# Float32r groups by single tiles, the first group copied out unnormalised, LayerNorm's tail in stages

## The chip, the cores and the metric

The kernel runs on one core of a Trainium2 chip. The metric is the device time of one execution in microseconds (us). Engines are TensorE (PE, matmuls; PEld is its weight load), VectorE (DVE), ScalarE (ACT), GpSimd (POOL) and SyncE (SP, which here only issues transfers). All run their own instruction streams in order and wait for each other by semaphores.

## The reference, cut to what matters

One layer on x of 512 tokens by 2048 channels, all in float32:

```
h = rms_norm(x) ; z = h @ w_in            # 2048 -> 7 x 1024
u = a_val * sigmoid(a_glu)                # mixer A
u = causal_depthwise_conv(u, width 31)
u = silu(layer_norm(u)) @ conv_pw_w + conv_pw_b ; y_a = u * silu(a_gate)
q, k = per-head rms_norm ; o = dilated_window_attention(q, k, v)   # 16 heads of 64
y_b = o * silu(b_gate)                    # mixer B
out = x + concat(y_a, y_b) @ w_out
```

## The kernel before, in words

Activations lie with channels on the 128 partitions and the 512 tokens along the row (x is passed transposed), so a matmul is 128x128 weights against 128x512 activations into one bank of PSUM. `GROUPS` lists 28 groups of 512 output columns. A *unit* is one group's weights for `KU` = 4 tiles of 128 input rows (1 MB), loaded into one of `RING` = 6 buffers `raw`. Units run in order; a group keeps four banks (`lin_ps`), m = 0 to 3, one for each 128 of its columns, and is evacuated (`evac`) when its last unit is done.

Each product is made of three matmuls on operands split in a high and a low part (`tri`, L361 to L365): high by high, high by low, low by high. From unit 8 on the parts are float16 of scaled weights (`split_hi` on ScalarE, `split_lo` on VectorE, one unit ahead) and of normalised x (`x16`, from `norm_x`). The first two groups (`vg` 0 and 1, units 0 to 7: conv value and gate columns) come before the row of 1/rms is known: their parts are float32r, of the raw weights (`exact_hi` L268, `exact_lo` L274) and of x times the norm's gain (`split_x` L311: hh and hl for even k, xr for odd). They are made two tiles of 128 rows at a time, half a unit ahead of use, in `PARTS` = 2 buffers, which the float16 parts use afterwards. These groups' banks are multiplied by `rrow` (1/rms of each token) on the way out (`evac_vg` L379).

Order is written out by hand. The time is counted in *steps* (`clock`): each unit has eight, and a step issues six matmuls. Before a step's matmuls the program emits what `after(n, fn)` has put into `calendar` for it, and the extras of that unit (`startup` L760 for units 0 to 7). Within an engine instructions run in the order of emission. The squares for the 1/rms are summed in `square_x`, turned into `rrow` by `token_rsqrt` (small matmuls L347, a power on GpSimd, a diagonal matrix on VectorE, a matmul L357); `norm_x` makes x16 afterwards.

The convolution and the LayerNorm behind it are a generator (`conv` L465). `run_conv` (L699) resumes it in a step when the planner's load of VectorE (180 plus the row length for each instruction, less `PACE` = 1200 a step) is below zero; the generator's `yield n` asks for n steps of rest. Its LayerNorm: sum of the eight tiles, mean by a matmul (L490), differences and squares, `token_rsqrt`, and a loop in which tile i is multiplied by 1/sigma (VectorE), goes through SiLU with gain and bias (ScalarE, L518), and tile i-2 is split into the float16 parts u16 (`split16` L296). The pointwise groups `pw` need all of u16. The attention heads run through the calendar at the same time: scores in three `s_ps` banks (L574, L575), exponentials on ScalarE (L584), values (L612). The scale of each later group's weights comes from sums of squares on ScalarE (`measure`, L182) and a small matmul (`bound`, L194).

At the start, SP issues all transfers in one list (L733 to L753): w tile 0, x0, w tile 1, x1, w tiles 2 and 3, x2 to x5, w tiles 4 and 5, and so on; GpSimd's queue loads the two gains qg and kg broadcast to 128 partitions (`load_consts` L147). Before the first real work `WARM` = 8 matmuls on zeros run.

Of the kernel before, what the change touches and what calls it, by code (L numbers as in the profile page):

```python
# [25 lines left out]
TAPS = 31  # L26
DH = 64
RING = 6
PARTS = 2
FIRST = 2  # L30
SLOTS = 37
LP = 4
WARM = 8
KU = 4
PERIOD = {0: 16, 1: 22}
START = 180
NORM_FROM = 32
PACE = 1200
RMS_EPS = 1e-6
LN_EPS = 1e-5  # L40
# [35 lines left out]
def layer(ctx: ExitStack, tc: tile.TileContext, xt, w1, w2, w3, g_in, conv_w, conv_b,  # L76
# [35 lines left out]
    def after(n, fn):  # L112

        calendar.setdefault(clock[0] + max(n, 1), []).append(fn)
# [32 lines left out]
    def load_consts():  # L147
        for t, src in ((cw, conv_w), (cb, conv_b), (lng, ln_g), (lnb, ln_b), (pwb, pw_b), (tab, table)):
            nc.sync.dma_start(t, src)
        for t, src in ((qg, q_g), (kg, k_g)):  # L150
            nc.gpsimd.dma_start(t, src.partition_broadcast(P))

# [112 lines left out]
            if i == mine[-1]:  # L265
                after(4, lambda: bound("w", sums.pop(group), lambda s, v: wscale.update({group: (s, v)})))

    def exact_hi(i, h, cuts=(0, 2)):  # L268

        wt = parts[i, h] = part_pool.tile([P, 2, 2, S], R32, name="wr", tag="part")  # L270
        for a, b in zip(cuts, cuts[1:]):
            A.activation(wt[:, 0, a:b], raw[i][:, 2 * h + a:2 * h + b], AF.Copy)

    def exact_lo(i, h, cuts=(0, 2)):  # L274
        wt = parts[i, h]
        for a, b in zip(cuts, cuts[1:]):
            V.tensor_tensor(wt[:, 1, a:b], raw[i][:, 2 * h + a:2 * h + b], wt[:, 0, a:b].bitcast(F32), op=OP.subtract)
        if h == 1:
            raw.pop(i)
            load(i + RING)  # L280
            after(max(9, 25 - 4 * i), lambda: measure(i + RING))

    def split_hi(i):
        if i < len(units):
            wt = part_pool.tile([P, 2, KU, S], F16, name="w16", tag="part")
            A.activation(wt[:, 0], raw[i], AF.Copy, scale=wscale[units[i][3:]][0])  # L286
            parts[i] = wt

    def split_lo(i):
        if i < len(units):  # L290
            wt = parts[i]
            V.scalar_tensor_tensor(wt[:, 1], raw.pop(i), wscale[units[i][3:]][0], wt[:, 0], op0=OP.mult, op1=OP.subtract)
            load(i + RING)
            after(9, lambda: measure(i + RING))

# [35 lines left out]
    def norm_x(k):  # L331

        t = temp("xn")
        V.scalar_tensor_tensor(t, xraw.pop(k), gs[:, k:k + 1], rrow, op0=OP.mult, op1=OP.mult)
        n = slots.tile([P, 2, S], F16, name="x16", tag="slot")
        A.activation(n[:, 0, :], t, AF.Copy)
        x16[k] = (n[:, 0, :], n[:, 1, :])
        after(2, lambda: V.tensor_tensor(n[:, 1, :], t, n[:, 0, :], op=OP.subtract))

    rstd = const.tile([P, NT], F32, name="rstd")  # L340
    rrow = slot("rrow")
# [37 lines left out]
    def evac_vg(g, m, ps):  # L379

        i = 2 * g + m // 2
        if m % 2 == 0:
            t = glu[i] = temp("glu")
            if g < FIRST:
                V.tensor_mul(t, ps, rrow)
                A.activation(t, t, AF.Sigmoid)
            else:
                A.activation(t, ps, AF.Sigmoid, scale=evac_scale(("vg", g)))
        else:
            t = u[i] = slot("u")  # L390
            if g < FIRST:
                V.tensor_mul(t, ps, rrow)
                V.tensor_mul(t, t, glu.pop(i))
            else:
                V.scalar_tensor_tensor(t, ps, evac_scale(("vg", g)), glu.pop(i), op0=OP.mult, op1=OP.mult)
# [69 lines left out]
    def conv():  # L465
# [27 lines left out]
        A.activation(mean_sb, mean, AF.Copy, scale=1.0 / C)  # L493
        yield 2
        acc2 = slot("lnacc2")
        sq = None
        for i in range(8):
            V.tensor_sub(cv[i], cv[i], mean_sb)
            if sq is not None:
                V.tensor_add(acc2, acc2, sq)  # L500
            if i == 0:
                A.activation(acc2, cv[i], AF.Square)
            else:
                sq = temp("lnsq")
                A.activation(sq, cv[i], AF.Square)
            yield 1
        yield 2
        V.tensor_add(acc2, acc2, sq)
        yield 5
        c = small.tile([P, NT], F32, name="lncol")  # L510
        row = temp("lnrow")
        for _ in token_rsqrt(acc2, C, LN_EPS, c, row):
# [2 lines left out]
        for i in range(8 + 2):  # L515
            if i < 8:
                V.tensor_mul(cv[i], cv[i], row)
                A.activation(cv[i], cv[i], AF.Silu, scale=lng[:, i:i + 1], bias=lnb[:, i:i + 1])  # L518
            if i >= 2:
                u16[i - 2] = split16(cv.pop(i - 2), scales["u"][0], "u16")  # L520
            yield 3


    pair, swapped, outs = {}, {}, {}
# [182 lines left out]

    banks = {}

    def slot_matmuls(i, m, half_i):  # L710

        kind, g = group = units[i][3:]
        first_u, last_u = i == of_group[group][0], i == of_group[group][-1]
        if first_u and half_i == 0:
            banks[group, m] = lin_ps.tile([P, S], F32, name="ps_l")
        ps = banks[group, m]
        ms = slice(m * P, (m + 1) * P)
        exact = i < n_exact
        wt = parts[i, half_i] if exact else parts[i]
        for kk in range(2):  # L720
            wk = kk if exact else 2 * half_i + kk
            k = units[i][2] * KU + 2 * half_i + kk
            act = xr[k] if exact else (u16 if kind == "pw" else y16 if kind in OUT_K else x16)[k]
            first, last = first_u and half_i == kk == 0, last_u and half_i == kk == 1
            if kind in ("q", "k", "v"):
                tri(ps, (act[0][:, ms], act[1][:, ms]), (wt[:, 0, wk, :], wt[:, 1, wk, :]), first, last)
            else:
                tri(ps, (wt[:, 0, wk, ms], wt[:, 1, wk, ms]), act, first, last)
        if last_u and half_i == 1:
            return lambda: evac(group, m, banks.pop((group, m)))  # L730

# [3 lines left out]
        load_part(0, k, k + 1)  # L735
        fetch_x(k)
    load_part(0, 2, 4)
    for k in range(2, 6):
        fetch_x(k)
    load(1, (0, 2))  # L740
    for k in range(6, 10):
        fetch_x(k)
    load_part(1, 2, 4)
    for k in range(10, 13):
# [6 lines left out]
    load_consts()  # L751
    for i in range(4, RING):
        load(i)  # L753
    exact_hi(0, 0, (0, 1, 2))
    exact_lo(0, 0, (0, 1, 2))
    split_x(0)
    split_x(1)
    square_x(0)

    def startup(h):  # L760

        lists = [[], [], [], []]
        if h < 7:
            lists[0].append(lambda: split_x(2 * h + 2))
            lists[2].append(lambda: split_x(2 * h + 3))
        for n, k in enumerate(k for k in range(1, KC) if (k - 1) * 6 // 15 == h):
            lists[n % 4].append(lambda k=k: square_x(k))
        i, hf = divmod(h + 1, 2)
        if h < 15:
            lists[0].append(lambda: exact_hi(i, hf))  # L770
            lists[1].append(lambda: exact_lo(i, hf))
        else:
            lists[1].append(lambda: split_lo(n_exact))
        if h == 14:
            lists[3].append(lambda: split_hi(n_exact))
        if h == 6:
            g = token_rsqrt(xacc, D, RMS_EPS, rstd, rrow)
            for n in (0, 1, 3):
                lists[n].append(lambda: next(g, None))
        if h == 4:  # L780
            lists[1].append(x_consts)
        if h == 5:
            lists[3].append(score_consts)
        if h == 9:
            lists[1].append(u_consts)
        for k in range(KC):
            n = NORM_FROM + k * (56 - NORM_FROM) // KC
            if n // 4 == h:
                lists[n % 4].append(lambda k=k: norm_x(k))
        return lists  # L790

    for i in range(len(units)):
        kind, g = group = units[i][3:]
        exact = i < n_exact
        if exact:
            order = [(m, hf) for hf in range(2) for m in range(4)]
            extra = startup(2 * i) + startup(2 * i + 1)
        else:
            order = [(m, hf) for m in range(4) for hf in range(2)]
            extra = [[] for _ in range(8)]  # L800
            extra[0].append(lambda: split_hi(i + 1))
            extra[2].append(lambda: split_lo(i + 1))
            if i + 1 < len(units) and units[i + 1][3] == "wb":
                for m in range(4):
                    extra[2 * m].append(lambda m=m: fetch_res(4 * units[i + 1][4] + m))
        if kind == "pw" and i == of_group[group][0]:
            while 7 not in u16:
                next(convolution)
        for n, (m, hf) in enumerate(order):
            clock[0] = 8 * i + n  # L810
            for fn in calendar.pop(clock[0], []) + extra[n]:
                fn()
            run_conv()
            done = slot_matmuls(i, m, hf)
            if done:
                done()
        if kind == "k" and i == of_group[group][-1]:
            attention(g)
# [47 lines left out]
```

## Time and profile before

| | us |
|---|---|
| median of 3 runs (lowest, highest) | 858.41 (856.31, 859.18) |
| the profiled execution | 856.66 |
| its span, first to last instruction | 854.7 |

The profile is of one execution. Busy shares of the span: PE 98%, VectorE 70%, ScalarE 58%, GpSimd 13%. In the chain of work that ended last PE has 95%. In rows of instructions the form is: engine, source line, operation, output<-inputs by the program's names, size. All VectorE instructions carry L71, the line of the helper that weighs them. A wait is put down to the instruction that came last before it ended.

### The profile page before, as it was taken

The numbers are of one execution on the slowest core, as the hardware profiler recorded it, in microseconds if no ns is written. First come the engines' busy times: TensorE is split into PE (matmuls) and PEld (weight loads), VectorE is DVE, ScalarE is ACT, GpSimd is POOL, SyncE is SP. The second block draws the span as 40 slices with busy tenths as digits, with TensorE's granted clock in tenths as the row PEclk, the third lists the DMA queues.
The fourth block names the chain that finished last, engine by engine and source line by source line (L and its number), as shares of the span: only waits on it lengthen the run. The fifth ranks groups of instructions, "written<-read, shape, count | busy, mean of one in ns | idle before, by whom it ended". The sixth has DMA issues, their size and how long they took to land.

```text
span 854.7 us, 10860 instructions
## 1 busy us (share of the span) xinstructions
PE 841.8 (98%) x4157; PEld 426.0 (50%) x4157; DVE 602.4 (70%) x968; ACT 499.6 (58%) x654; POOL 114.1 (13%) x165
## 2 busy tenths in 40 slices
PE   8999999999999999999999999997999999999998
PEld 5878744444444444444444444443444444444443
DVE  5778689888898988788787767536537577545353
ACT  6647554443645466668667667868777774544110
POOL 0010010101413011004222102010101010111100
PEclk9999999999999999999999999999999999999999
DMA  9922322232353534443737543423335565341022
GB/s 311 349 80 75 144 99 99 99 110 101 103 167 90 169 118 134 105 117 102 199 115 173 154 130 87 142 94 86 114 121 137 169 225 166 106 122 50 2 99 98
DMA packets 79748, 110.24 MB, mean 129 GB/s; under 512 B 62256, under 2 KB 62640, under 8 KB 70480
## 3 DMA queue, kind: packets, MB, share of 16 engines
q1 hardware_dynamic: 78320, 107.24, 40.6%
q0 software_dynamic: 1088, 2.16, 1.0%
q8 instruction: 32, 0.52, 0.2%
q14 instruction: 20, 0.16, 0.1%
q10 hardware_dynamic: 288, 0.14, 0.1%
HBM read 88.56 MB, written 4.19 MB: 109 GB/s over the span
## 4 chain that ended last, share of the span: by engine, by line
PE 95%; ACT 3%; DMA 1%; issue 1%; DVE 1%; SPq 0%; DVEq 0%; ACTq 0%
PE ps_l L363 30%; PE ps_l L364 30%; PE ps_l L365 30%; PE ps_o L612 2%; PE ps_s L574 1%; PE ps_s L575 1%; DMA x<-xt_dram 1%; ACT junk L182 0%; ACT cv L518 0%; ACT u L299 0%; ACT sx L584 0%; DVE w L71 0%; ACT w L286 0%; DVE cv L71 0%; ACT gate L404 0%
## 5 line engine op out<-in xcount | busy, mean ns | idle before, releaser
L286 ACT ACTIVATE w<-wf,ws 128x2048 f16<-128x2048 f32 x68 | 136.1, 2002 | 169.8 <-PE ps_l L365 167.1
L71 DVE SCALAR_TENSOR_TENSOR w<-wf,ws,w 128x2048 f16<-128x2048 f32 x68 | 159.7, 2349 | 40.5 <-ACT w L286 40.4
L71 DVE SCALAR_TENSOR_TENSOR cv<-u,cw,cv 128x511 f32<-128x511 f32 (+14 forms) x240 | 160.2, 730 | 0.3 <-ACT cv L472 0.3
L364 PE MATMUL ps_l<-w,x 128*128 128x512 f16 x384 | 145.5, 379 | 0.0
L365 PE MATMUL ps_l<-w,x 128*128 128x512 f16 x384 | 145.5, 379 | 0.0
L365 PE MATMUL ps_l<-x,w 128*128 128x512 f16 x384 | 145.5, 379 | 0.0
L364 PE MATMUL ps_l<-x,w 128*128 128x512 f16 x384 | 145.5, 379 | 0.0
L363 PE MATMUL ps_l<-w,x 128*128 128x512 f16 x384 | 145.5, 379 | 0.0
L363 PE MATMUL ps_l<-x,w 128*128 128x512 f16 x384 | 145.5, 379 | 0.0
L182 ACT ACTIVATE junk<-wf 128x2048 bf16<-128x2048 f32 x68 | 129.2, 1900 | 2.3 <-DMA wf<-w_dram 2.1
L365 PEld LDWEIGHTS <-w 128*128 128x128 f16 x704 | 68.8, 98 | 83.1
L363 PEld LDWEIGHTS <-w 128*128 128x128 f16 x704 | 68.9, 98 | 82.1 <-issue 3.5
L364 PEld LDWEIGHTS <-w 128*128 128x128 f16 x704 | 68.8, 98 | 77.3 <-issue 0.7
L365 PE MATMUL ps_l<-y,w 128*128 128x512 f16 x256 | 97.0, 379 | 0.0
L364 PE MATMUL ps_l<-y,w 128*128 128x512 f16 x256 | 97.0, 379 | 0.0
L363 PE MATMUL ps_l<-y,w 128*128 128x512 f16 x256 | 97.0, 379 | 0.0
L71 DVE SCALAR_TENSOR_TENSOR res<-ps_l,esc,res 128x512 f32<-128x512 f32 (+1 forms) x49 | 36.0, 737 | 59.2 <-PE ps_l L365 51.4
L196 POOL TENSOR_SCALAR ws<-ws 128x1 f32<-128x1 f32 x26 | 9.4, 362 | 462.8 <-DVE ws L71 462.8
L365 PEld LDWEIGHTS <-x 128*128 128x128 f16 x384 | 37.6, 98 | 45.3
L363 PEld LDWEIGHTS <-x 128*128 128x128 f16 x384 | 37.6, 98 | 43.0
L364 PEld LDWEIGHTS <-x 128*128 128x128 f16 x384 | 37.6, 98 | 42.5
L71 DVE CUSTOM_DVE_ANT_0 sx<-ps_s,tab 128x128 f32<-128x128 f32 (+1 forms) x64 | 30.7, 487 | 33.3 <-PE ps_s L575 18.5
(185 smaller groups left out, 1044.6 us busy)
## 6 DMA issues: line engine op xcount, KB each, us to landing
wf<-w_dram SPq DMA_DIRECT2D x72, 1024.0 KB, 4.9
x<-xt_dram SPq DMA_DIRECT2D x16, 256.0 KB, 6.6
res<-xt_dram SPq DMA_DIRECT2D x16, 256.0 KB, 5.4
out_dram<-res SPq DMA_DIRECT2D x15, 256.0 KB, 2.0
wf<-w_dram SPq DMA_DIRECT2D x7, 512.0 KB, 7.2
kb<-k POOLq DMA_DIRECT2D x32, 64.0 KB, 3.8
wf<-w_dram SPq DMA_DIRECT2D x2, 256.0 KB, 3.7
tab<-table_dram SPq DMA_DIRECT2D x1, 256.0 KB, 4.0
```

The costliest lines, as they stand in the source:

```text
L71: return getattr(self.engine, name)(out, src, *args, **kw)
L182: A.activation(junk[:, :n], src, AF.Square, scale=scale, accum_out=acc)
L196: G.tensor_scalar(scale, scale, 1e-30, 2.0 ** (-2 * top), op0=OP.max, op1=OP.mult)
L286: A.activation(wt[:, 0], raw[i], AF.Copy, scale=wscale[units[i][3:]][0])
L363: T.matmul(ps, ah, bh, start=first, stop=False)
L364: T.matmul(ps, ah, bl, start=False, stop=False)
L365: T.matmul(ps, al, bh, start=False, stop=last)
L574: T.matmul(ps[:, :w], q[:, i * P:w], k[:, :w], start=True, stop=False)
L575: T.matmul(ps[:, :w], q[:, i * P:w], swapped[hd][:, :w], start=False, stop=True)
L612: T.matmul(po[:, i * P:(i + 1) * P], v2[j // 2][:, j % 2, h8, :], got["t"][:, part * (ALL // P) + FROM[i] // P + j, :], start=(j == 0 and ...
```

## The change

The float32r groups go by single tiles. Tile n is one weight tile (unit n // 4, row block n % 4) with high and low part in one of four buffers of half the size; the float16 units use two of these, one for each part. `exact_matmuls(n)` issues half a tile's twelve matmuls in a step, so a tile takes two steps: all high by high, then high weight by low x, then low weight by high x, over the four banks in turn; for the first and last tile of a group (but not the very first) it is sorted by bank instead. Parts of tile s+3 and x of tile s+2 are made in the steps of tile s. At the start weights and x alternate: tile 0, x0, tile 1, x1, tile 2. In SP's list w tiles 4 and 5 come ahead of x4 and x5. The broadcast loads of qg and kg go to step 12, the other pieces of the start get their own steps, and the normalising of x runs from step 37 to 70 instead of 32 to 56, with its high part a step after the multiplication and the low part a step later than it was. Nine warming matmuls.

The first group is copied out of its banks by ScalarE as it is; seven steps later it is multiplied by `rrow`, nine steps later comes the sigmoid, eleven later the product u. The second group is unchanged.

In LayerNorm the running sum stays two squares behind instead of one, with more rest between, and in the last loop SiLU follows one stage behind the multiplication, and the split two steps after that.

```diff
-PARTS = 2
+PARTS = 4
-WARM = 8
+WARM = 9
-NORM_FROM = 32
+NORM_FROM = 37
...
+    def exact_hi(n):
+        i, k = divmod(n, KU)
+        wt = parts[i, k] = part_pool.tile([P, 2, S], R32, name="wr", tag="part")
+        A.activation(wt[:, 0], raw[i][:, k], AF.Copy)
+    def exact_lo(n):
+        i, k = divmod(n, KU)
+        wt = parts[i, k]
+        V.tensor_tensor(wt[:, 1], raw[i][:, k], wt[:, 0].bitcast(F32), op=OP.subtract)
+        if k == KU - 1:
             raw.pop(i)
             load(i + RING)
-            after(max(9, 25 - 4 * i), lambda: measure(i + RING))
+            after(max(6, 25 - 4 * i), lambda: measure(i + RING))
...
+            parts[i] = [part_pool.tile([P, KU, S], F16, name=n, tag="part") for n in ("wh", "wl")]
+            A.activation(parts[i][0], raw[i], AF.Copy, scale=wscale[units[i][3:]][0])
...
-        after(2, lambda: V.tensor_tensor(n[:, 1, :], t, n[:, 0, :], op=OP.subtract))
+        after(1, lambda: A.activation(n[:, 0, :], t, AF.Copy))
+        after(3, lambda: V.tensor_tensor(n[:, 1, :], t, n[:, 0, :], op=OP.subtract))
...
+        if g == 0:
+            t = u[i, m % 2] = temp("glu") if m % 2 == 0 else slot("u")
+            A.activation(t, ps, AF.Copy)
+            def finish():
+                V.tensor_mul(t, t, u.pop((i, 0)))
+                u[i] = u.pop((i, 1))
+            after(7, lambda: V.tensor_mul(t, t, rrow))
+            if m % 2 == 0:
+                after(9, lambda: A.activation(t, t, AF.Sigmoid))
+            else:
+                after(11, finish)
...
-            if sq is not None:
-                V.tensor_add(acc2, acc2, sq)
+            if len(squares) > 1:
+                V.tensor_add(acc2, acc2, squares.pop(0))
...
+            yield 1 + i % 2
+        while squares:
             yield 1
-        yield 2
-        V.tensor_add(acc2, acc2, sq)
-        yield 5
+            V.tensor_add(acc2, acc2, squares.pop(0))
+        yield 4
...
                 V.tensor_mul(cv[i], cv[i], row)
-                A.activation(cv[i], cv[i], AF.Silu, scale=lng[:, i:i + 1], bias=lnb[:, i:i + 1])
+            if 1 <= i < 8 + 1:
+                A.activation(cv[i - 1], cv[i - 1], AF.Silu, scale=lng[:, i - 1:i], bias=lnb[:, i - 1:i])
+            yield 2
             if i >= 2:
                 u16[i - 2] = split16(cv.pop(i - 2), scales["u"][0], "u16")
-            yield 3
+            yield 1
...
+    def exact_matmuls(n):
+        s, second = divmod(n, 2)
+        i, kk = divmod(s, KU)
+        k = s % KC
+        group = units[i][3:]
+        wt, xk = parts[i, kk], xr[k]
+        terms = [(m, a, b) for a, b in ((0, 0), (0, 1), (1, 0)) for m in range(4)]
+        if s and k in (0, KC - 1):
+            terms = sorted(terms)
+        for m, a, b in terms[6 * second:][:6]:
+            if k == 0 and a == b == 0:
+                banks[group, m] = lin_ps.tile([P, S], F32, name="ps_l")
+            T.matmul(banks[group, m], wt[:, a, m * P:(m + 1) * P], xk[b], start=k == 0 and a == b == 0,
+                     stop=k == KC - 1 and a == 1)
+            if k == KC - 1 and a == 1:
+                evac(group, m, banks.pop((group, m)))
...
-    for k in range(2, 6):
+    for k in range(2, 4):
         fetch_x(k)
     load(1, (0, 2))
-    for k in range(6, 10):
+    for k in range(4, 10):
...
-    exact_hi(0, 0, (0, 1, 2))
-    exact_lo(0, 0, (0, 1, 2))
-    split_x(0)
-    split_x(1)
+    for n in range(2):
+        exact_hi(n)
+        exact_lo(n)
+        split_x(n)
+    exact_hi(2)
+    exact_lo(2)
     square_x(0)
...
+    def startup(n):
+        s, second = divmod(n, 2)
+        todo = []
+        if not second:
+            if s + 3 < KU * n_exact:
+                todo += [lambda: exact_hi(s + 3), lambda: exact_lo(s + 3)]
+            if s + 2 < KC:
+                todo.append(lambda: split_x(s + 2))
+        if n == 0:
+            for k in range(1, KC):
+                after(4 + (k - 1) * 26 // 14, lambda k=k: square_x(k))
+            for k in range(KC):
+                after(NORM_FROM + k * (70 - NORM_FROM) // KC, lambda k=k: norm_x(k))
+            g = token_rsqrt(xacc, D, RMS_EPS, rstd, rrow)
+            for m in (32, 33, 35):
+                after(m, lambda: next(g, None))
+            for m, fn in ((12, load_norms), (21, x_consts), (40, score_consts), (37, u_consts)):
+                after(m, fn)
+            after(8 * n_exact - 4, lambda: split_hi(n_exact))
+            after(8 * n_exact - 3, lambda: split_lo(n_exact))
+        return todo
```

## Rows read from the trace of the kernel before

**Rows 1.** The page's busy times, TensorE: busy us (share of the span) xinstructions.
```profile
PE 841.8 (98%) x4157; PEld 426.0 (50%) x4157; DVE 602.4 (70%) x968; ACT 499.6 (58%) x654; POOL 114.1 (13%) x165
```

**Rows 2.** Stretches: from:to, length, busy us of PE, PEld, DVE, ACT, POOL; clock, DMA share, GB/s.
```profile
0.00:10.00 10.00, 5.75 (x12) 1.98 (x12) 2.76 (x7) 4.29 (x7) 1.99 (x9) 1.00 0.75 213
10.00:20.00 10.00, 10.00 (x36) 7.68 (x37) 7.88 (x11) 8.51 (x14) 0.00 (x0) 1.00 1.04 398
...
560.00:600.00 40.00, 35.37 (x190) 17.05 (x189) 21.31 (x40) 31.49 (x43) 5.31 (x7) 1.00 0.30 82
```

**Rows 3.** Waits of TensorE over the whole span: total us, times, longest.
```profile
PE ps_l L363 <- ACT hh L319: 3.0, 1, 3.0
PE ps_s L194 <- ACT junk L182: 2.4, 1, 2.4
PE ps_s L574 <- DVE st L71: 2.2, 1, 2.2
```

**Rows 4.** Timeline of TensorE, 0 to 15 us: start, us, instruction [idle before].
```profile
0.98 3.59 PE L138 MATMUL ps_s<-wz 128*128 128x512 f16 x8 [0.98 <-POOL wz L135]
7.59 0.80 PE L363 MATMUL ps_l<-hh,wr 128*128 128x512 f32 x1 [3.01 <-ACT hh L319]
...
9.85 0.79 PE L363 MATMUL ps_l<-xr,wr 128*128 128x512 f32 x1 [0.26 <-ACT xr L319]
...
12.51 0.63 PE L365 MATMUL ps_l<-hh,wr 128*128 128x512 f32 x1
12.94 0.58 PE L363 MATMUL ps_l<-xr,wr 128*128 128x512 f32 x1
13.35 0.40 PE L364 MATMUL ps_l<-xr,wr 128*128 128x512 f32 x1
13.59 0.39 PE L365 MATMUL ps_l<-xr,wr 128*128 128x512 f32 x1
```

**Rows 5.** Timeline of ScalarE, 6 to 7 us.
```profile
6.29 0.63 ACT L272 ACTIVATE wr<-wf 128x512 fp32r<-128x512 f32 x1 [2.06 <-DMA wf<-w_dram]
6.83 0.71 ACT L319 ACTIVATE hh<-x,gcol 128x512 fp32r<-128x512 f32 x1
```

**Rows 6.** DMA issues made in 1.1 to 1.6 us, then 2.1 to 2.6: KB, us to landing.
```profile
x<-xt_dram SPq DMA_DIRECT2D x1, 256.0 KB, 4.2
...
x<-xt_dram SPq DMA_DIRECT2D x1, 256.0 KB, 6.9
```

**Rows 7.** DMA queues: all from 3.0 to 4.3 us; then all and GpSimd's, 4.3 to 7.2.
```profile
DMA packets 230, 0.42 MB, mean 325 GB/s; under 512 B 24, under 2 KB 24, under 8 KB 230
...
DMA packets 249, 0.45 MB, mean 157 GB/s; under 512 B 49, under 2 KB 49, under 8 KB 249
...
q0 software_dynamic: 50, 0.06, 43.5%
```

**Rows 8.** Timeline of ScalarE: a copy of two weight tiles at once.
```profile
16.80 1.06 ACT L272 ACTIVATE wr<-wf 128x1024 fp32r<-128x1024 f32 x1 [0.69 <-PE ps_l L365]
```

**Rows 9.** Timeline of TensorE where the bank changes (at 41.86).
```profile
41.63 0.39 PE L365 MATMUL ps_l<-xr,wr 128*128 128x512 f32 x1
41.86 0.40 PE L363 MATMUL ps_l<-hh,wr 128*128 128x512 f32 x1
```

**Rows 10.** Timelines at the change to float16: VectorE's low part, TensorE's first use.
```profile
99.23 2.35 DVE L71 SCALAR_TENSOR_TENSOR w<-wf,ws,w 128x2048 f16<-128x2048 f32 x1
...
102.52 0.39 PE L363 MATMUL ps_l<-x,w 128*128 128x512 f16 x1
```

**Rows 11.** Waits, 540 to 620 us: total, times, longest.
```profile
DVE u L71 <- ACT u L299: 15.1, 6, 5.6
ACT cv L518 <- DVE cv L71: 10.3, 5, 3.4
```

**Rows 12.** Tile u (u16 is part of it): durations, first and last start.
```profile
L363 PE MATMUL ps_l<-u,w x64: 376/379/379, 635.2 to 678.3; 128*128 128x512 f16 x64
...
L71 DVE SCALAR_TENSOR_TENSOR u<-cv,us,u x8: 746/750/752, 576.2 to 608.8; 128x512 f16<-128x512 f32 x8
```

More of the change, by code (lines that the diff above doesn't have):

```diff
@@ L149, in load_consts, with load_norms @@
             nc.sync.dma_start(t, src)
+    def load_norms():
         for t, src in ((qg, q_g), (kg, k_g)):
@@ L266, in measure @@
                 after(4, lambda: bound("w", sums.pop(group), lambda s, v: wscale.update({group: (s, v)})))
[L268 to L278, printed above, removed]
+    def exact_hi(n):
[7 more added lines that the diff above has]
+        if k == KU - 1:
             raw.pop(i)
             load(i + RING)
-            after(max(9, 25 - 4 * i), lambda: measure(i + RING))
+            after(max(6, 25 - 4 * i), lambda: measure(i + RING))
     def split_hi(i):
         if i < len(units):
-            wt = part_pool.tile([P, 2, KU, S], F16, name="w16", tag="part")
-            A.activation(wt[:, 0], raw[i], AF.Copy, scale=wscale[units[i][3:]][0])
-            parts[i] = wt
+            parts[i] = [part_pool.tile([P, KU, S], F16, name=n, tag="part") for n in ("wh", "wl")]
+            A.activation(parts[i][0], raw[i], AF.Copy, scale=wscale[units[i][3:]][0])
     def split_lo(i):
         if i < len(units):
-            wt = parts[i]
-            V.scalar_tensor_tensor(wt[:, 1], raw.pop(i), wscale[units[i][3:]][0], wt[:, 0], op0=OP.mult, op1=OP.subtract)
+            wh, wl = parts[i]
+            V.scalar_tensor_tensor(wl, raw.pop(i), wscale[units[i][3:]][0], wh, op0=OP.mult, op1=OP.subtract)
             load(i + RING)
@@ L335, in norm_x @@
         n = slots.tile([P, 2, S], F16, name="x16", tag="slot")
-        A.activation(n[:, 0, :], t, AF.Copy)
         x16[k] = (n[:, 0, :], n[:, 1, :])
-        after(2, lambda: V.tensor_tensor(n[:, 1, :], t, n[:, 0, :], op=OP.subtract))
+        after(1, lambda: A.activation(n[:, 0, :], t, AF.Copy))
+        after(3, lambda: V.tensor_tensor(n[:, 1, :], t, n[:, 0, :], op=OP.subtract))
     rstd = const.tile([P, NT], F32, name="rstd")
@@ L381, in evac_vg @@
         i = 2 * g + m // 2
-        if m % 2 == 0:
+        if g == 0:
[9 more added lines that the diff above has]
+                after(11, finish)
+        elif m % 2 == 0:
             t = glu[i] = temp("glu")
@@ L495, in conv @@
         acc2 = slot("lnacc2")
-        sq = None
+        squares = []
         for i in range(8):
             V.tensor_sub(cv[i], cv[i], mean_sb)
-            if sq is not None:
-                V.tensor_add(acc2, acc2, sq)
+            if len(squares) > 1:
+                V.tensor_add(acc2, acc2, squares.pop(0))
             if i == 0:
@@ L503, in conv @@
             else:
-                sq = temp("lnsq")
-                A.activation(sq, cv[i], AF.Square)
+                squares.append(temp("lnsq"))
+                A.activation(squares[-1], cv[i], AF.Square)
+            yield 1 + i % 2
+        while squares:
             yield 1
-        yield 2
-        V.tensor_add(acc2, acc2, sq)
-        yield 5
+            V.tensor_add(acc2, acc2, squares.pop(0))
+        yield 4
         c = small.tile([P, NT], F32, name="lncol")
@@ L717, in slot_matmuls @@
         ms = slice(m * P, (m + 1) * P)
-        exact = i < n_exact
-        wt = parts[i, half_i] if exact else parts[i]
+        wh, wl = parts[i]
         for kk in range(2):
-            wk = kk if exact else 2 * half_i + kk
-            k = units[i][2] * KU + 2 * half_i + kk
-            act = xr[k] if exact else (u16 if kind == "pw" else y16 if kind in OUT_K else x16)[k]
+            wk = 2 * half_i + kk
+            k = units[i][2] * KU + wk
+            act = (u16 if kind == "pw" else y16 if kind in OUT_K else x16)[k]
             first, last = first_u and half_i == kk == 0, last_u and half_i == kk == 1
             if kind in ("q", "k", "v"):
-                tri(ps, (act[0][:, ms], act[1][:, ms]), (wt[:, 0, wk, :], wt[:, 1, wk, :]), first, last)
+                tri(ps, (act[0][:, ms], act[1][:, ms]), (wh[:, wk, :], wl[:, wk, :]), first, last)
             else:
-                tri(ps, (wt[:, 0, wk, ms], wt[:, 1, wk, ms]), act, first, last)
+                tri(ps, (wh[:, wk, ms], wl[:, wk, ms]), act, first, last)
         if last_u and half_i == 1:
@@ L753, in layer @@
         load(i)
-    exact_hi(0, 0, (0, 1, 2))
-    exact_lo(0, 0, (0, 1, 2))
-    split_x(0)
-    split_x(1)
-    square_x(0)
[L760 to L776, printed above, removed]
-            g = token_rsqrt(xacc, D, RMS_EPS, rstd, rrow)
[L778 to L790, printed above, removed]
@@ L795, in layer @@
         if exact:
-            order = [(m, hf) for hf in range(2) for m in range(4)]
-            extra = startup(2 * i) + startup(2 * i + 1)
+            order = [(None, None)] * 8
         else:
@@ L810, in layer @@
             clock[0] = 8 * i + n
-            for fn in calendar.pop(clock[0], []) + extra[n]:
+            if exact:
+                extra = {n: startup(clock[0])}
+            due = calendar.pop(clock[0], [])
+            for fn in extra[n] + due if exact else due + extra[n]:
                 fn()
             run_conv()
-            done = slot_matmuls(i, m, hf)
+            done = exact_matmuls(clock[0]) if exact else slot_matmuls(i, m, hf)
             if done:
```

## The prediction

> **What bounds the kernel now.** I read first the page's busy times [rows 1]: TensorE (PE) is busy for 841.8 us of a span of 854.7, so any change that does not shorten PE's own stream can give back at most 12.9 us. The table of stretches [rows 2] says where these are: 4.25 us idle in the first ten, 4.63 between 560 and 600, and nearly all of the rest behind the last matmul, which the change does not touch. From 10 to 20 us, where transfers run at 398 GB/s, PE is never idle, and no wait of it falls between that and the second place. PE's waits [rows 3] name the causes: 3.0 us for the first x part (hh, from ScalarE), then 2.4 us for a square sum of ScalarE (L194) and 2.2 us for VectorE to free a score bank (L574). The second place is where LayerNorm's tail runs. Third, the timeline of PE at the start [rows 4]: eight warming matmuls end at 4.57, the first real one starts at 7.59, the second triple at 9.85, and the pitch is 0.43 us (12.51 to 12.94) until 13.35, from where it is 0.23. Ten matmuls start before 13.35. At 0.43 us for 512 columns the array runs at the lower of its two levels (1.2 GHz), at 0.23 at the upper (2.4); the granted-clock column shows 1.00 throughout and does not tell them apart. So the start costs PE more than the idle time says: it stands still until 7.59, with only ten matmuls done by 13.35.
>
> **The start.** Four edits act here: one tile of 128 rows instead of two as the unit, x0 split between the first and second weight tile, twelve matmuls of k=0 before any of k=1, and the two broadcast loads on GpSimd's queue put off. Before, ScalarE copies the second weight tile at 6.29, for which it had waited 2.06 us, and only then makes hh of x0 at 6.83 [rows 5], although x0, issued at about 1.2, landed 4.2 us later, at 5.4 [rows 6]. After, hh of x0 is next in line: 5.4 + 0.71 = 6.1 for the first matmul even if no transfer becomes faster. The second gain is the broadcast: between 3.0 and 4.3 us the DMA engines move 325 GB/s, between 4.3 and 7.2 only 157, while the software queue's 50 packets hold 43.5% of the engines' time [rows 7], that is 0.435 x 2.9 = 1.26 us of each engine. Without them x0 lands up to 1.26 us earlier (first matmul at 4.9), or no earlier if it had passed already (6.1). I take the middle, 5.5.
> From there twelve matmuls need only tile 0 and x0: 12 x 0.43 = 5.2 us, until 10.7, or less if the clock rises first. Tile 1 needs x1, which before landed 6.9 us after an issue at about 2.1 [rows 6], at 9.0: ready at 9.8, so the stop of 0.26 us before 9.85 goes as well.
> When the pitch falls is the open term. Before it fell 3.5 us after the last stop (9.85) and 5.8 us after the first real matmul (7.59). From 5.5 this is 9.0 to 11.3; I take the middle, 10.2. By then (10.2 - 5.5)/0.43 = 10.9 matmuls are done, a count which before was reached at 13.35 + 0.9 x 0.23 = 13.6. Gain 3.4 us. Ends: start at 4.9 with the fall at 8.4 gives 4.5; start at 6.1 with the fall at 11.9 gives 13.5 matmuls, 14.2 before, so 2.3.
> What could be late next is tile 2 or 3. The order on SP's queue moves w tiles 4 and 5 ahead of x4 and x5, half a megabyte that at 398 GB/s is 1.3 us for these two, which are needed after more than 15 us. ScalarE's copy for tile s+3 must wait until PE leaves tile s-1, whose buffer it takes, and behind it in ScalarE's queue stands the split of x for tile s+2; that is at least one tile (2.8 us) ahead of its use, against 1.4 us of ScalarE work (0.63 + 0.71). No cost; if x2 came no earlier than before, at most about 1 us.
> The broadcast loads themselves return on the same queue at step 12, where the engines still move w tiles; they take the same 1.26 us there, which tiles loaded more than ten microseconds ahead of their use absorb, and their readers come at step 40.
>
> **The groups in float32r.** 384 matmuls before and after. Two copies of 0.63 in place of one of 1.06 [rows 5, 8] are 0.1 us more per tile on ScalarE, on VectorE about as little: some 3 us over 90, hidden, as neither is full (ScalarE 8.51 of 10 us even in its densest stretch [rows 2]). A new thing is that consecutive matmuls go to four banks in turn. Where the bank changes now, as at 41.86, the pitch is the same 0.23 as inside a bank [rows 9]; the trace has no stretch in which every matmul changes it. I take nothing, with 0 to +21 ns a matmul (0 to 8 us) as the ends that matter.
> The group's last tile is sorted by bank, as is the next group's first, so bank m has nine matmuls (2.1 us) between its end and its next use, where it had eighteen. ScalarE empties one in about 0.6, without waiting for the row of 1/rms; in its queue stand one weight copy and one square (1.25 us) in front, so the first bank is free after about 1.9 us of 2.8 counted from the step's start. No stall; if a square sum of 1.9 us stood there, one of about 1 us. Putting the normalisation off removes no PE wait, as there was none.
> At the change to float16 the low part of unit 8 is ready at 99.23 + 2.35 = 101.6, for a first use at 102.52 [rows 10]: 0.9 us. With two smaller buffers its high part can start one tile earlier. This can only help.
>
> **LayerNorm's tail.** Before, each stage emits the multiply on VectorE and the SiLU that reads it at once; so ScalarE, whose queue is in order, stood for VectorE 10.3 us in five waits, and VectorE then 15.1 us in six for the high parts that followed [rows 11]. The square sums and score banks behind these were late, and PE waited 2.4 and 2.2 [rows 3]. After, SiLU i-1 is emitted one stage (three steps, about 4 us) behind its multiply, so these waits should go, with 10.3 us of ScalarE time against a backlog of about 10 (six steps of lead used up, plus 2.4). Both PE stalls go: 4.6 us. The other end is 0: the two squares in flight make that part three steps longer, the last low part comes two steps later, and convolution falls some five steps behind by the code's own budget of 1200 a step, since the first group's u is ready 11 steps after its matmuls and the later normalising of x uses the same budget. Together some ten steps, 13 us. The last low part was written at 609.5 for a first use at 635.2 [rows 12]: 26 us of room, of which 13 stay, so the pointwise groups still do not wait. But the tail meets other heads and unit splits than before; a low part of 2.35 us in front of LayerNorm's diagonal matrix would stop PE by up to 2.4 us. Range -2.4 to 4.6; I take 4.6, since the removed waits are the named cause of the whole.
>
> **Sum.** 3.4 + 4.6 = 8.0 us off the profiled run's 856.66 (its span of 854.7 and 2.0 around it), so 848.7. That run is 1.75 below the median of 858.41; from the median the forecast is 850.4 us.
>
> **Rivals.**
> *Only the start pays.* Stalls of the same size come back at another place of 530 to 620 us. For it: ScalarE is busy 31.49 of 40 us there [rows 2] and its table switches stay. Against: idle waits, not work, made the backlog. 858.4 - 3.4 = 855.0 (853.9 to 856.1).
> *Only the tail pays:* the transfers, not the order, set the first matmuls, or PE stops again between tiles 1 and 3 and the clock rises late, so about 1 us of the start stays. For it: x1 landed only at 9.0. 858.4 - 5.6 = 852.8.
> *Neither does what it says*, 857 to 859.
> *Slower: the change of bank at every matmul costs pitch or clock.* Place: the 384 matmuls from 5 to 100 us. It decides from 8.0/384 = 21 ns a matmul, or from 40 matmuls at 0.43. If half of them ran at 0.43 it would be 192 x 0.2 = 38 us more, near 889; at 35 ns a matmul, 858.4 - 8.0 + 13.4 = 863.8. Against it: one bank change in six now costs nothing [rows 9].
> The Trainium skill speaks for this rival: "TensorE: Matmul & The Clock Gate", section "A second HAM failure mode: psum-queue depth-cycling", has a kernel that went round its PSUM banks and whose clock swung between its levels, since PE idled briefly between groups; by that rule the stretch would run at a mixed pitch, towards the 889 above. The page blames the small idle times, and no run here shows such a swing: PE is busy 10.00 of 10.00 us from 10 to 20 [rows 2], banks changing.
>
> **How the numbers follow.** Forecast 0.55, only the start 0.22, only the tail 0.08, neither 0.06, slower 0.09. About 0.3% (2.6 us, so 855.8) is what a measurement can tell from no change. Faster is most of the first three: 0.53 + 0.17 + 0.07 = 0.77; the same 0.14; slower 0.09. The range runs from both gains at their best (858.4 - 4.5 - 4.6 = 849.3, less 2 us of spread between runs, 847) to the weak end of the start alone with a small new stop, 857.
>
> **What would show it.** Right: first real matmul between 4.9 and 6.1 us, pitch of 0.23 from about 10, no idle PE between 5 and 100, the SiLU's waits gone, PE busy all of 560 to 600. Wrong: a float32r pitch above 0.25 past 13 us, PE waiting for ScalarE's copies of group 0 near 50 us, for x between tiles 1 and 4, or for u in front of the pointwise groups.

## The result and the profile after

The changed kernel takes 848.19 us (median of four runs, 847.18 to 848.84) against 857.36 before (856.23 to 859.18): ratio 0.989, 95% interval 0.9866 to 0.9914, 9.2 us less. The forecast was 850.4 from a median of 858.41, 8.0 less. The two profiled executions differ by 7.8 us (856.66 and 848.84; spans 854.7 and 846.9). That the medians differ by 1.4 more lies within the spread of the runs of before, 3 us.

First the page's busy times and then TensorE's waits over the whole span of the changed kernel, to be compared with [rows 1] and [rows 3]:

```profile
PE 839.3 (99%) x4158; PEld 425.5 (50%) x4158; DVE 603.5 (71%) x983; ACT 502.2 (59%) x673; POOL 117.3 (14%) x165
```

```profile
PE ps_l L741 <- ACT xr L320: 1.9, 1, 1.9
PE ps_s L138 <- POOL wz L135: 1.0, 1, 1.0
PE ps_l L741 <- ACT hh L320: 0.7, 1, 0.7
```

The two stalls of 2.4 and 2.2 us are gone, the wait for hh has shrunk from 3.0 to 0.7, and a stop of 1.9 us for x1 (xr) is new. The table of stretches of the changed kernel has the same columns as [rows 2]:

```profile
0.00:10.00 10.00, 6.51 (x21) 3.31 (x21) 2.67 (x6) 4.19 (x6) 1.99 (x9) 1.00 0.74 208
10.00:20.00 10.00, 9.95 (x36) 8.00 (x37) 7.55 (x12) 7.21 (x14) 0.00 (x0) 0.83 1.04 396
...
560.00:600.00 40.00, 40.00 (x219) 19.52 (x218) 23.43 (x40) 33.01 (x49) 5.39 (x7) 1.00 0.36 102
```

Where the 7.8 us came from is read off two instructions. The first float16 matmul started at 102.52 [rows 10] and starts at 99.60 now, so the part in front of it gave 2.9 us:

```profile
99.60 0.39 PE L364 MATMUL ps_l<-x,wh 128*128 128x512 f16 x1
```

Of these 2.9, the first two tiles account for 2.1: the 25th float32r matmul, with which tile 2 begins, started at 16.60 before (first row below) and at 14.51 after (second row). The other 0.8 came behind it: from there to the first float16 matmul are 85.92 us before and 85.09 after, with the same 360 float32r matmuls and the same small ones, so a float32r matmul takes some 2 ns less on average.

```profile
16.60 0.40 PE L363 MATMUL ps_l<-hh,wr 128*128 128x512 f32 x1
```

```profile
14.51 1.10 PE L741 MATMUL ps_l<-hh,wr 128*128 128x512 f32 x4
```

The first pointwise matmul started at 635.2 [rows 12]; now, from the view of tile u:

```profile
L364 PE MATMUL ps_l<-u,wh x64: 376/379/380, 627.5 to 670.5; 128*128 128x512 f16 x64
...
L71 DVE SCALAR_TENSOR_TENSOR u<-cv,us,u x8: 731/748/752, 579.7 to 613.7; 128x512 f16<-128x512 f32 x8
```

That is 7.7 us earlier, so 4.8 lie between, where 4.63 us of idle PE were. Behind it nothing changed.

The start also differs between profiles of the same start code. In the five profiles with the start of before (before, and e1, e5, e6 and e7 of the experiments below) the first float16 matmul comes at 102.5 to 104.6 us, 103.7 in the mean; in the four with the new start (after, and e2_again, e8 and e9) at 98.8 to 100.6, 99.8 in the mean. The profile of before is the earliest of its five, so 2.9 is at the low side, and 3.9 is the difference of the means.

The start is not what I had described. TensorE's timeline of the changed kernel (compare [rows 4]):

```profile
5.17 1.18 PE L741 MATMUL ps_l<-hh,wr 128*128 128x512 f32 x4 [0.66 <-ACT hh L320]
6.18 1.07 PE L741 MATMUL ps_l<-hl,wr 128*128 128x512 f32 x4
7.08 1.07 PE L741 MATMUL ps_l<-hh,wr 128*128 128x512 f32 x4
10.05 4.62 PE L741 MATMUL ps_l<-xr,wr 128*128 128x512 f32 x12 [1.90 <-ACT xr L320]
```

Tile 0's twelve matmuls run at about 0.24 us each, where the first ones of before had 0.43; then PE stops, and tile 1's twelve need 4.46 us (10.05 to 14.51), 0.37 each. The table of stretches shows the clock there: 0.50 granted, the lower level, and nearly 1.00 again from 14 on.

```profile
9.00:10.00 1.00, 0.00 (x0) 0.00 (x0) 0.00 (x0) 0.72 (x1) 0.00 (x0) 1.00 1.05 416
11.00:12.00 1.00, 1.00 (x4) 0.81 (x3) 0.69 (x1) 1.00 (x3) 0.00 (x0) 0.50 1.04 406
...
14.00:15.00 1.00, 1.00 (x6) 0.82 (x5) 1.00 (x2) 0.81 (x2) 0.00 (x0) 0.95 1.05 391
```

The cause of the stop is in GpSimd's timeline and in the DMA queues from 4.3 to 7.2 us (compare [rows 7]):

```profile
1.43 0.77 POOL L153 DMA_DIRECT2D qg<-q_g_dram  x1 [0.18 <-issue]
2.19 0.56 POOL L153 DMA_DIRECT2D kg<-k_g_dram  x1
```

```profile
DMA packets 185, 0.34 MB, mean 117 GB/s; under 512 B 37, under 2 KB 37, under 8 KB 185
...
q0 software_dynamic: 43, 0.05, 34.5%
```

The broadcast loads go out at the same moment as before. They are emitted at step 12, but GpSimd has nothing else in front of them and nothing to wait for, so its queue reaches them at once. The dip in the transfers stays, and x1 lands at 9.26.

Two executions among the experiments, the profiled one of e2_start_only (1101.16 us) and one of e9_warm8 (1431.67 us), ran at a mean granted clock of 0.75 and 0.58 and are left out of the numbers below; e2_again is e2_start_only's kernel, profiled once more.

### The profile page after: what moved, and what is told of

The parts are those of the page before. It is cut to its first block, busy times and chain, and to the rows that moved or that the text cites. A ratio compares the mean times of both kernels' runs of the same rounds, so it can differ in the third digit from the quotient of the medians.

```text
span 846.9 us, 10899 instructions
## 1 busy us (share of the span) xinstructions
PE 839.3 (99%) x4158; PEld 425.5 (50%) x4158; DVE 603.5 (71%) x983; ACT 502.2 (59%) x673; POOL 117.3 (14%) x165
## 4 chain that ended last, share of the span: by engine, by line
PE 98%; DMA 1%; SPq 0%; ACT 0%; DVE 0%; DVEq 0%; issue 0%
PE ps_l L364 28%; PE ps_l L365 28%; PE ps_l L366 28%; PE ps_l L741 10%; PE ps_o L629 2%; PE ps_s L591 1%; PE ps_s L592 1%; DMA x<-xt_dram 1%; PE ps_s L358 0%; PE ps_s L348 0%; PE ps_s L504 0%; SPq L257 0%; ACT xr L320 0%; DVE res L71 0%; SPq L310 0%; DVEq L892 0%
## 5 line engine op out<-in xcount | busy, mean ns | idle before, releaser
L288 ACT ACTIVATE wh<-wf,ws 128x2048 f16<-128x2048 f32 x68 | 135.9, 1998 | 160.9 <-PE ps_l L365 154.9
L71 DVE SCALAR_TENSOR_TENSOR wl<-wf,ws,wh 128x2048 f16<-128x2048 f32 x68 | 159.7, 2348 | 39.3 <-ACT wh L288 39.1
L366 PE MATMUL ps_l<-x,wl 128*128 128x512 f16 x384 | 145.6, 379 | 0.0
L366 PE MATMUL ps_l<-wh,x 128*128 128x512 f16 x384 | 145.6, 379 | 0.0
L365 PE MATMUL ps_l<-wl,x 128*128 128x512 f16 x384 | 145.6, 379 | 0.0
L364 PE MATMUL ps_l<-x,wh 128*128 128x512 f16 x384 | 145.6, 379 | 0.0
L364 PE MATMUL ps_l<-wh,x 128*128 128x512 f16 x384 | 145.6, 379 | 0.0
L365 PE MATMUL ps_l<-x,wh 128*128 128x512 f16 x384 | 145.6, 379 | 0.0
L366 PEld LDWEIGHTS <-wl 128*128 128x128 f16 x704 | 68.8, 98 | 83.1
L364 PEld LDWEIGHTS <-wh 128*128 128x128 f16 x704 | 68.9, 98 | 79.7 <-issue 0.7
L365 PEld LDWEIGHTS <-wh 128*128 128x128 f16 x704 | 68.8, 98 | 77.5 <-issue 0.7
L366 PE MATMUL ps_l<-y,wl 128*128 128x512 f16 x256 | 97.1, 379 | 0.0
L365 PE MATMUL ps_l<-y,wh 128*128 128x512 f16 x256 | 97.0, 379 | 0.0
L364 PE MATMUL ps_l<-y,wh 128*128 128x512 f16 x256 | 97.0, 379 | 0.0
```

The source lines that it names most:

```text
L71: return getattr(self.engine, name)(out, src, *args, **kw)
L288: A.activation(parts[i][0], raw[i], AF.Copy, scale=wscale[units[i][3:]][0])
L364: T.matmul(ps, ah, bh, start=first, stop=False)
L365: T.matmul(ps, ah, bl, start=False, stop=False)
L366: T.matmul(ps, al, bh, start=False, stop=last)
```

## The experiments

Ratios are to the kernel before, run beside each experiment on the same chip, with a 95% interval.

**LayerNorm's edits alone, and the rest alone.** e1_ln_only is the kernel before with the edits to the squares and to the last loop; e2_start_only is the changed kernel with these undone.

> The kernel before with LayerNorm's edits alone (squares two behind, SiLU a stage behind its multiply). Theory (in-order waits): ScalarE's 10.3 us of waits before the SiLU fall under 3, PE's stalls of 2.4 and 2.2 us between 560 and 600 us go, the start stays as before (first real matmul 7.59): about 4.6 us less than before, ratio 0.9946. Rival (the tail only meets other heads because everything in front came earlier): the edits alone leave stalls of about the same size, no more than 1 us less.

> The changed kernel with LayerNorm's edits undone, so single tiles, copy-out, new start. Theory: the last float32r matmul ends near 99.6 us (102.5 before) and the stalls of 4.6 us between 550 and 600 stay or return near by: about 2.9 us less than before, ratio 0.9966. Rival (shift): the convolution's later place alone ends the stalls, so 7 to 8 us less, ratio 0.991.

> The changed kernel with LayerNorm's edits undone, once more for its profile at the full clock, since its time (848.4 us) was that of the changed kernel with these edits (848.2). By the shift theory (formed from that time) the trace shows no PE wait between 540 and 620 us although SiLU still follows its multiply at once and ScalarE still waits for VectorE there, several us in all. By the theory of the prediction the two stalls of 2.4 and 2.2 us are still there and the time was gained elsewhere.

e1_ln_only: 852.77 us, ratio 0.994 (0.9925 to 0.9954), 5.3 us less; no wait of ScalarE before SiLU is left, no PE wait between 540 and 620. The tail went as the theory had it; the start did not, as the first real matmul came at 9.39 us in this profile and not at 7.59, with the same start code. e2_start_only: 848.29 us, ratio 0.9889 (0.9872 to 0.9905), 9.8 us less, where the theory had 2.9 and the rival 7 to 8. The two parts together give 9.2 and alone 5.3 and 9.8, so part of the gain is the same in both: either part alone ends the two stalls. In e2_again's waits between 540 and 630 us ScalarE still stands for VectorE:

```profile
DVE u L71 <- ACT u L300: 12.8, 7, 4.4
...
ACT cv L532 <- DVE cv L71: 4.3, 2, 2.2
```

PE, however, waits nowhere between 550 and 600, and once for 0.6 us after that, for a head's transfer:

```profile
550.00:600.00 50.00, 50.00 (x273) 24.83 (x272) 28.35 (x54) 38.73 (x52) 6.05 (x8) 1.00 0.42 114
```

So SiLU's waits need not stop PE, and the prediction's account of the stalls was in doubt. The shift theory came in its place: what decides is where the tail stands among the heads and the unit splits.

**Which of LayerNorm's edits, or only the place.** Three kernels made from the one before: the last loop alone, the squares alone, and neither but a rest.

```diff
--- e7_shift5: all there is to it
+        yield 5
         for i in range(8 + 2):
```

> The kernel before with the last loop alone changed: SiLU one stage behind its multiply, split two steps later; the loop begins at the same step. Theory of the prediction (waits behind an in-order queue): ScalarE's waits before SiLU under 3 us, both PE stalls gone, 4.6 us less (853.5). Rival (place): the loop stands where it stood among the heads, so stalls of 2 us or more stay.

> The kernel before with the squares alone changed (sum two behind, more rest), which moves the last loop, itself as before, some three steps back. Theory of the prediction: ScalarE's waits before SiLU stay near 10 us and so do the stalls, same time (858). Rival (place): 3 to 5 us less.

> The kernel before with five steps of rest in front of LayerNorm's last loop and nothing else. Theory of the prediction: waits before SiLU and stalls as before, 858. Rival (place alone decides): no PE stall from 540 to 620 us, 4 to 5 us less, 853.5.

Measured: 852.73 us (0.9935, 0.9912 to 0.9959), 853.35 (0.9944, 0.9927 to 0.9962) and 853.12 (0.9942, 0.9921 to 0.9964). Each alone gives 4.3 to 5 us, and none of the three has a PE wait between 540 and 620. Waits of ScalarE before SiLU in e6_squares_only, then in e7_shift5 (total, times, longest):

```profile
ACT cv L519 <- DVE cv L71: 8.0, 3, 3.7
```

```profile
ACT cv L519 <- DVE cv L71: 4.3, 2, 2.3
```

e5_silu_only has none. The place of the loop is read from its first multiply on VectorE (first the kernel before, then e7_shift5) and from the first pointwise matmul:

```profile
L71 DVE TENSOR_TENSOR cv<-cv,lnrow x8: 661/684/691, 559.7 to 597.9; 128x512 f32<-128x512 f32 x8
```

```profile
L71 DVE TENSOR_TENSOR cv<-cv,lnrow x8: 660/684/694, 570.6 to 600.1; 128x512 f32<-128x512 f32 x8
```

The loop of e5_silu_only stands where it stood before: from the loop's first multiply to the first pointwise matmul are 70.6 us (560.6 to 631.2), in the kernel before 75.5 (559.7 to 635.2) with 4.6 of stalls in them. In e6_squares_only it is 68.9 (563.6 to 632.5), in e7_shift5 61.6 (570.6 to 632.2). So each theory is right that its cause is enough, and wrong that the other is not. Staging SiLU ends the stalls at the old place. Moving the unstaged loop ends them too, by 2.0 us with the squares' edit (70.9 to 68.9, with 8.0 us of waits left) or by 9.3 with the rest alone. In e2_again the unstaged loop stands 59.7 us in front of the first pointwise matmul (567.6 to 627.3), so the changed kernel's other edits had moved it about as far as the rest in e7. An earlier or later start alone does not end the stalls: both are there, 2.4 and 2.2 us, in e3_before_bcast_sp and e10_reorder_only, whose float32r parts end at 100.4 and 103.3. The stalls needed both, the backlog and the place; which instruction of a head or a split met the tail there, no run separates.

**The broadcast loads.** The same one-line edit on the kernel before and on the changed one puts them into SyncE's list, where they really come later (at 24.4 us in e3, at 27.9 in e4):

```diff
-            nc.gpsimd.dma_start(t, src.partition_broadcast(P))
+            nc.sync.dma_start(t, src.partition_broadcast(P))
```

> The kernel before, with the broadcast loads of qg and kg issued from SyncE's list, where the constants are, instead of GpSimd's queue; nothing else. Theory (the broadcast slows the first tiles): the dip to 157 GB/s between 4.3 and 7.2 us goes, x1 lands before 7.8 us instead of 9.0 and w tile 1 before 5.5 instead of 6.3, the first real matmul starts near 6.5 instead of 7.59, no stop near 9.85: 1 to 3 us less in all. Rival (the dip is the queue of plain transfers itself): landings and first matmul as before, same time.

> The changed kernel with the two broadcast loads issued from SyncE's list at the same step 12. In the changed kernel's trace GpSimd still issued them at 1.43 and 2.19 us, since nothing in its queue made it wait, x1 landed at 9.26, PE stopped for 1.9 us and then ran at a granted clock of 0.50 from 10.8 to about 14. Theory: x1 lands before 7.5, no stop of more than 0.3 us at tile 1, no fall of the clock, last float32r matmul about 3.4 us earlier (96.2 instead of 99.6), 3.4 us less than the changed kernel, ratio to before about 0.985. Rival (plain transfers alone set x1, or PE stops later instead, at tile 2 or 3): less than 1 us gained on the changed kernel.

e3_before_bcast_sp: 854.66 us, ratio 0.9963 (0.9951 to 0.9974), 3.4 us less, a little more than the 1 to 3 expected. From 4.3 to 7.2 us the engines now move 309 GB/s, w tile 1 lands 3.4 us after its issue, the first real matmul starts at 6.33, and the float32r part ends at 100.4. e4_after_bcast_sp: 845.57 us, ratio 0.9854 (0.9838 to 0.987), so 12.5 us below the kernel before and 2.6 below the changed one (by medians not taken side by side; the profiled runs differ by 3.2); it is the fastest of all. Its DMA queues from 4.3 to 7.2 us and TensorE's timeline:

```profile
DMA packets 360, 0.87 MB, mean 300 GB/s; under 512 B 39, under 2 KB 39, under 8 KB 360
```

```profile
5.16 1.67 PE L741 MATMUL ps_l<-hh,wr 128*128 128x512 f32 x4 [0.15 <-ACT hh L320]
6.66 1.07 PE L741 MATMUL ps_l<-hl,wr 128*128 128x512 f32 x4
7.57 1.07 PE L741 MATMUL ps_l<-hh,wr 128*128 128x512 f32 x4
8.57 3.05 PE L741 MATMUL ps_l<-xr,wr 128*128 128x512 f32 x12
```

No stop before tile 1, and the granted clock stays at 1.00 in every microsecond from 10 to 14, where the changed kernel had 0.50. x1 lands at 7.8 (7.5 expected). The float32r part ends at 96.59, 3.0 earlier than in the changed kernel (3.4 expected). So the two loads cost the start this much, in both kernels. The edit changes two things at once, the time of the loads and the queue that issues them; which of the two counts is not separated.

**What made the start faster.** e10_reorder_only gives the kernel before the new order of the first four copies and splits, still with two tiles to a step.

> The kernel before with its first operations in the order weight tile 0, x0, weight tile 1, x1, nothing else: steps still need two tiles. Theory (single tiles make the gain, as twelve matmuls need only the first): first real matmul near 5.2, but after three matmuls PE stops until x1 is split, near 10, as before; the float32r part ends within 1 us of where it did (102.5), time 857 to 858. Rival (order makes the gain): 2 to 3 us less.

857.85 us, ratio 0.9991 (0.9977 to 1.0005): nothing. Its timeline shows why:

```profile
5.17 0.51 PE L363 MATMUL ps_l<-hh,wr 128*128 128x512 f32 x1 [0.59 <-ACT hh L319]
5.95 0.51 PE L364 MATMUL ps_l<-hl,wr 128*128 128x512 f32 x1 [0.28 <-DVE hl L71]
6.30 0.39 PE L365 MATMUL ps_l<-hh,wr 128*128 128x512 f32 x1
9.98 0.79 PE L363 MATMUL ps_l<-xr,wr 128*128 128x512 f32 x1 [3.29 <-ACT xr L319]
```

The first matmul comes 2.4 us earlier, and after three PE stands for x1, with 3.29 us of new waiting. Single tiles make the gain: twelve matmuls in place of three can run before x1 is there. x1 lands at 9.2 here and at 9.3 in the changed kernel, but tile 2 begins at 17.36 here and at 14.51 there, 2.9 us earlier. The other edits of the start, as SyncE's order, were not run alone.

**The order of banks.** e8_sorted keeps each tile's matmuls together by bank.

```diff
-        if s and k in (0, KC - 1):
-            terms = sorted(terms)
+        terms = sorted(terms)
```

> The changed kernel with each tile's twelve matmuls sorted by bank (three in a row into each) instead of going round the four banks. In the changed kernel twelve matmuls took 2.77 us (96.83 to 99.60), 0.231 each, against 0.233 before. Theory (banks in turn cost nothing): pitch within 3 ns of 0.231, time within 1.5 us of the changed kernel's 848.2. Rival (going round the banks costs): pitch falls below 0.225, 3 us or more less. Rival (it gains): pitch back at 0.233, 1 us more.

848.98 us, ratio 0.9877 (0.9848 to 0.9906), the changed kernel's time within the interval. The twelve matmuls named in the expectation do not test it: they are the group's last tile, sorted by bank in both kernels. The tile in front of it does, first in the changed kernel, then here:

```profile
94.06 1.09 PE L741 MATMUL ps_l<-hh,wr 128*128 128x512 f32 x4
...
96.83 2.93 PE L741 MATMUL ps_l<-xr,wr 128*128 128x512 f32 x12
```

```profile
95.08 0.40 PE L740 MATMUL ps_l<-hh,wr 128*128 128x512 f32 x1
...
97.85 2.93 PE L740 MATMUL ps_l<-xr,wr 128*128 128x512 f32 x12
```

It takes 2.77 us in both, 0.231 a matmul. From the start of tile 2 to the first float16 matmul are 85.09 us in turn and 85.08 sorted (15.55 to 100.63): no cost and no gain in the steady part. At its start e8_sorted needs the low parts sooner and shows two small waits of 0.3 us for them.

**The ninth warming matmul.**

> The changed kernel with eight warming matmuls instead of nine. Theory (the stop at tile 1 decides the clock): same start, same time, 848.2 within 1 us. Rival (the ninth bridges to the first real matmul and lifts the clock before it): first twelve matmuls at 0.43 instead of 0.25, tile 0 done near 10.3, about 1 to 2 us more.

849.04 us, ratio 0.9879 (0.985 to 0.9907). First real matmul at 5.15, tile 0 at about 0.25 us a matmul, nearly as in the changed kernel's profile (0.24). The ninth does nothing that can be measured here.

**The two losses by one line each.** e11_two_lines is the kernel before with the rest of e7 and the queue of e3.

> The kernel before with two one-line edits: the broadcast loads from SyncE's list, and five steps of rest in front of LayerNorm's last loop. Theory (two separate losses, at the start and in the tail): 3.4 + 4.7 = 8 us less than before, near 850, no PE wait from 540 to 620 us and the float32r part ending near 100.4. Rival (the earlier start moves the tail against the heads again): a stall of 2 us or more returns, 852 or more.

850.24 us, ratio 0.9901 (0.9868 to 0.9934), 7.8 us less, no PE wait between 540 and 620. The losses add (3.4 and 4.6 alone), and two lines give most of what the whole change gives. The float32r part ended later than expected, at 101.2; the start varies from run to run.

## Why the prediction was right, point by point

**The time.** 9.2 us less against 8.0 forecast, inside the range. In the pair of profiles the tail gave 4.8 (forecast 4.6) and all in front of the float16 matmuls 2.9 (forecast 3.4 for the start, bounds 2.3 to 4.5). Of the 2.9 only 2.1 is the start itself, which is below the forecast's weak end; the other 0.8 is the float32r pitch, for which nothing was taken. By the means over all profiles the start gave about 3. The upper bound of 4.5 is a slip of its own sum: 8.1 matmuls by 8.4 were reached before at 12.6, which gives 4.2.

**The start: right in sum, by errors that cancel.** Luck has a part in the size. The step "hh of x0 is next in line" holds: 5.17 us, between 4.9 and 6.1. Wrong was "the two broadcast loads put off": moving the emission moved nothing. The earlier x0 that I had expected from it came without it: x0 landed 3.1 us after its issue here, and 3.0 to 3.2 in all later profiles, also with the start of before (e1), not 4.2. Wrong was "the stop goes as well": it is 1.90 us, and the clock falls behind it. And wrong was the slow pitch for all of tile 0: 0.24 us was measured. The warming burst ended 0.66 us before it, not 3.0 as before, but that this is the reason is not shown: in e2_again, with the same start code, the burst ended 0.11 us before, and the first four matmuls took 0.46 us each. Ten matmuls were counted for 13.35; the changed kernel has twelve done by 8.2, loses 1.9 to the stop and 1.7 to the slow pitch behind it (12 x (0.37 - 0.23)). Two of the prediction's own signs of being wrong are therefore there, a pitch above 0.25 past 13 us and PE waiting for x at tile 1, and the time came out all the same. How the broadcast would act if it were really moved is shown by e3 and e4: x1 lands 1.4 to 1.8 us earlier, where 1.26 was counted for x0, and the whole is worth about 3 us.

**No cost in float32r: right, with a small gain not foreseen.** Twelve matmuls take 2.77 us (94.06 to 96.83, 0.231 each), slightly below the 0.233 of before, which makes the 0.8 us named above. The order of the banks is not its cause, as e8_sorted has it too; the cause is open. The rival of the banks falls with this and with e8_sorted. The Trainium skill's rule on cycling through banks ("TensorE: Matmul & The Clock Gate", section "A second HAM failure mode: psum-queue depth-cycling") blames small idle times of PE; here there are none while the banks go round, from 20 to 100 us the granted clock is 1.00, and the one fall of the clock follows the stop of 1.90 us for a transfer.

**The copies of group 0: right.** ScalarE's timeline has the weight copy and the square in front, as counted, and then the copies; PE does not wait.

```profile
50.80 0.63 ACT L274 ACTIVATE wr<-wf 128x512 fp32r<-128x512 f32 x1 [1.61 <-PE ps_l L741]
51.34 0.62 ACT L329 ACTIVATE xsq<-x 128x512 f32<-128x512 f32 x1
51.86 0.58 ACT L385 ACTIVATE glu<-ps_l 128x512 f32<-128x512 f32 x1
```

**The change to float16: right.** The low part starts at 94.32 and is ready at 96.7, 2.9 us ahead of the first float16 matmul at 99.60, where it was 0.9.

**LayerNorm's tail: right in size, its attribution only half.** "The removed waits are the named cause of the whole" was the step that failed. The waits before SiLU do go, and that is enough (e5_silu_only); but the new place of the tail, which I had listed as a risk, would have been enough without it (e2_again, e6, e7). In the changed kernel both act, so LayerNorm's edits are worth nothing there that could be measured: with them 848.2, without them 848.3. The room for the pointwise groups came out as counted, 627.5 - 614.4 = 13.1 us left of 26.

**The rivals.** "Only the start pays" looked at the wrong pair: the start's part did pay 9.8 us alone, but with the stalls ended by its shift. "Only the tail pays" had its condition met (a stop between tiles 0 and 1, the clock late) without its price.

## What to carry to other kernels

An instruction that is emitted later is not issued later if its queue is empty and it waits for nothing (the broadcast loads went out at 1.43 and 2.2 us in both kernels): to put a transfer off, place it behind other work of its queue, and look in the trace at when it went out. When a stall goes, shift the old code by a few steps before crediting the edit: here three different edits each ended the same 4.6 us, and their gains do not add. At a start bound by transfers, count the matmuls that can run on the first pair of tiles; making more of them possible was worth more than making the first one earlier.

## What the runs showed of the hardware that was not expected

A stop of PE of 1.90 us after some 3 us of matmuls was followed by a granted clock of 0.50 from about 10.7 to 14 us, and the same came behind stops of 1.79 and 2.26 us in e8 and e9, while in e4, with no such stop, it stayed at 1.00. The stop does not decide alone: in e2_again a stop of 1.77 us had twelve matmuls at 0.24 us each behind it, at a granted clock of 1.00.

```profile
10.75 3.02 PE L738 MATMUL ps_l<-xr,wr 128*128 128x512 f32 x12 [1.77 <-ACT xr L320]
```

What else decides is not shown. In the kernel before the records show 1.00 over its first fourteen microseconds although the pitch was 0.43, so at a start the pitch is the better witness. Two broadcast loads of 32 KB from GpSimd's queue, 0.07 MB in all, cost 3.4 us in one kernel and about 3 in the other (2.6 by the medians, 3.2 by the profiled runs). From 4.3 to 7.2 us the DMA engines move 105 to 157 GB/s with them and 300 to 316 without. W tile 1, issued just behind the first of them, landed from 4.6 to 7.6 us after its issue in the profiles with the broadcast on GpSimd's queue, and from 3.4 to 4.5 in the three without it.
